# Splitting the first weight tile of the second MLP ahead of a norm, in a two-layer decoder on one core

## The chip, the cores and the metric

The kernel runs on one core of one Trainium2 chip. The metric is the device time of one execution in microseconds. The core has five engines, each with an instruction queue of its own: TensorE (PE; its weight loads are listed as PEld), VectorE (DVE), ScalarE (ACT), GpSimd (POOL) and SyncE (SP), which here issues most of the DMAs.

## The reference

A decoder of two layers works on 512 tokens of width 1024 (`x`), in fp32. Each layer has a mixer and an MLP, each behind an RMS norm whose scale and shift come from a conditioning vector (`mod`, six vectors of 1024 for each layer), and each added to `x` through a gate. Layer 0 mixes by pooling, layer 1 by a gated unit (SGU). The part around the change is the end of layer 1's mixer and the start of its MLP:

```python
    gated = u * mixed.reshape(B_, S_, SGU_WIDTH)
    return gated @ w_out
...
        x = x + g1[:, None, :] * y
        h = modulate(rmsnorm(x, norm_mlp_g[i]), sh2, sc2)
        x = x + g2[:, None, :] * sq_relu_mlp(h, mlp_w1[i], mlp_w2[i])
...
def sq_relu_mlp(h, w1, w2):
    return jnp.square(jax.nn.relu(h @ w1)) @ w2
```

## The kernel before

**Products in three parts.** Each fp32 operand of the large products is split into a high half (rounded, on ScalarE) and a low half (the rest, on VectorE); `mm3` (L174) then issues three matmuls, low weight by high input (L176), high weight by low input (L177), high by high (L178). A weight tile of 128 x 1024 (512 KB) is loaded by `raw4` (L153) and split by `split` (L164): high half `wh` by L167, low half `wl` by L168. `parts` (L590) does the same for inputs (L592 high, L593 low).

**Buffers.** Raw weight tiles, the tiles of the modulation columns (`ada`) and the scaled rows of a norm (`xs`) go round in one pool, `w4`, of three buffers: the fourth tile asked for takes the place of the first, and its load waits until that one has been read. `wh` and `wl` have five buffers each, PSUM has two pools of four banks (`ps`, `xz`).

**Order.** TensorE's instructions keep the order of the program. Those of ScalarE, VectorE, GpSimd and SP are put in order by the framework's scheduler, outside the first stage; on the chip each engine then works through its list in that order, and an instruction that waits holds up those behind it.

**The end of the mixer.** The tokens are in four tiles `t` of 128, the width in two halves `dh` of 512. For each `dh` the four blocks of `w_o` are loaded and split (`blocks`, L1028), and for each `t` 24 matmuls make a product `po` of 128 x 512. `gated` (L959) multiplies it by the gate (L964), adds it to `x` (L965), takes the sum of squares of the new half row on ScalarE (L969) and adds the sums (L973). After some of the token tiles `ada_tile` (L191) loads one modulation tile and reduces it on VectorE (L198, L183); GpSimd builds diagonals `dgu` from the results (L207).

**The norm.** `normed(hf, i, n)` (L980) norms 256 tokens, those of tiles 2hf and 2hf+1. GpSimd takes the power -1/2 (L223), ScalarE scales the two row tiles (L985, `xs`), TensorE turns them in 16 transposes (L992, `px`), VectorE and ScalarE apply scale and shift (L999, L997, into `h32`), and `parts` writes the two halves of the MLP's input `hb`, in four pairs of `k` (eight blocks `k` of 128 channels). `spill(hf)` (L1006) has GpSimd copy these tokens' `x` to memory (`xd`). For the first 256 tokens this stands in the gated output at `dh == 1`, after `t == 2`, so that TensorE works on `t == 3` while the first half is normed.

**The start of the MLP.** `first1` (L1130) loads and splits the first n = 4 tiles of `w1f` (tiles 0 to 3, each for 128 columns of the hidden width), multiplies them with the first 256 tokens, norms the second 256 after the third tile, then does tile 3's first half and all four tiles' second halves. Tiles 4 to 7 follow as units of `mlp` (L595): `f_prep` (L638) loads and splits them some units ahead. SP also loads the first tiles of the second weights there, `bt` and two of `b`, 1024 KB each (L761).

Of the kernel before, what the change touches and what calls it, by code (L numbers as in the profile page):

```python
# [78 lines left out]
def decoder_kernel(ctx: ExitStack, tc: tile.TileContext, xtok, vecs, rows, fgrow, ada0, adag, ada1, pool_w, w1s, w1, w1f, w1b, w2, w2e, w_v, w_u, w_o, wsT, lnp, bs, out):  # L79
# [23 lines left out]
    def f32(t):  # L103
        return t.bitcast(F32)
# [34 lines left out]
    def X(t):  # L139
        return x_[t // 2][:, t % 2]  # L140
# [8 lines left out]
    def mod(i, c):  # L149
        return mods[i][:, c : c + 1]  # L150


    def raw4(src):  # L153
        r = w4.tile([P, D], F32, name="raw", tag="w4")
        nc.sync.dma_start(r, src)
        return r
# [4 lines left out]
    def wpair():  # L161
        return wtile("wh"), wtile("wl")

    def split(r):  # L164

        h, l = wpair()
        A.activation(h, r, AF.Copy)  # L167
        V.tensor_tensor(l, r, f32(h), ALU.subtract)  # L168
        return h, l
# [63 lines left out]
    with (  # L233
# [67 lines left out]
        def rms():  # L301
            v0 = sm.tile([P, NT], F32, name="rv4", tag="rv4")
            V.tensor_scalar(v0, ss, RMS_EPS, None, ALU.add)
            rt.append(power(v0, NT))
# [270 lines left out]
    def ytile(name):  # L575
        return vy.tile([P, NT, D], F32, name=name, tag="y")
# [403 lines left out]
    def normed(hf, i, n):  # L980

        xs = []
        for r in range(2):
            t = w4.tile([P, D], F32, name="xs", tag="w4")
            A.activation(t, X(2 * hf + r), AF.Copy, scale=rms(2 * hf + r))  # L985
            xs.append(t)
        c = slice(256 * hf, 256 * hf + 256)
        for k in range(0, KD, 2):
            px = bank("px")
            for q in range(2):  # L990
                for r in range(2):
                    T.transpose(px[:, 256 * q + P * r : 256 * q + P * r + P], xs[r][:, P * (k + q) : P * (k + q) + P], ident)  # L992
            tt = h32[0][:, k : k + 2, c] if h32 else sm.tile([P, 2, 256], F32, name="tt", tag="tmp")
            for q in range(2):
                a, b = scl[i][n][:, k + q : k + q + 1], mod(i, c_sh(n, k + q))
                if q:
                    A.activation(tt[:, q], px[:, 256:512], AF.Identity, bias=b, scale=a)  # L997
                else:
                    V.tensor_scalar(tt[:, q], px[:, 0:256], a, b, ALU.mult, ALU.add)  # L999
            parts(H(slice(k, k + 2), c), tt)  # L1000
# [32 lines left out]
    with (  # L1033
        tc.tile_pool(name="lp", bufs=1) as lp,
        tc.tile_pool(name="up", bufs=8) as up,
        tc.tile_pool(name="gp", bufs=8) as gp,
        tc.tile_pool(name="ur", bufs=2) as ur,
    ):
        v4 = ytile("v")
        vt = [v4[:, t].rearrange("p (a b) -> p a b", a=2) for t in range(NT)]  # L1040
        lnt = lp.tile([P, 2, D], F32, name="lnt")
        wb = lp.tile([P, 2, HEADS, P], F32, name="wsbs")
        nc.sync.dma_start(lnt, lnp.rearrange("(o a b) -> o a b", o=1, a=2).to_broadcast([P, 2, D]))
        nc.sync.dma_start(wb[:, 0], wsT)
        nc.sync.dma_start(wb[:, 1], bs.rearrange("(o a b) -> o a b", o=1, a=HEADS).to_broadcast([P, HEADS, P]))
        G.affine_select(
            out=wb[:, 0], in_=wb[:, 0], compare_op=ALU.is_ge, fill=0.0, base=0, pattern=[[0, HEADS], [1, P]], channel_multiplier=-1
        )
        for ch in range(2):
            wv = blocks(w_v[ch])  # L1050
            for hf in range(2):
                ts = (2 * hf, 2 * hf + 1)
                pos = {t: bank("po", xz) for t in ts}
                for k in range(KD):
                    for t in ts:
                        mm3(pos[t], H(k, tok[t]), wv(k), k == 0, k == KD - 1)
                    if k == LATE and (ch, hf) == (0, 0):
                        normed(1, 1, 0)
                for t in ts:
                    A.activation(vt[t][:, ch], pos[t], AF.Gelu)  # L1060
        for t in range(NT):
            v = vt[t]
            stt = sm.tile([P, 2, V.BN_STATS_DIM], F32, name="stt", tag="stt")
            for ch in range(2):
                V.bn_stats(stt[:, ch, :], v[:, ch])
            ag = sm.tile([P, V.BN_AGGR_DIM], F32, name="ag", tag="ag")
            V.bn_aggr(ag, stt)
            r = rsqrt(ag[:, 1:2], 1.0, LN_EPS, 1)
            V.tensor_scalar(v, v, ag[:, 0:1], r, ALU.subtract, ALU.mult)
            for n, op in ((0, ALU.mult), (1, ALU.add)):  # L1070
                V.tensor_tensor(v, v, lnt[:, n].rearrange("p (a b) -> p a b", a=2), op)

        u, gt, wu = {}, {}, {}
        ex = [lambda: spread_cols(mods[1][:, c_g(0, 0) : c_g(0, 0) + KD])]
        ex += [lambda q=q: ada_tile(1, q, ada1[8 + q], get4) for q in range(24, 40)]

        def do_u(n):
            for q in range(n, min(n + 3, KD)):
                if q not in wu:
                    r = ur.tile([P, D], F32, name="ur", tag="ur")  # L1080
                    nc.sync.dma_start(r, w_u[q])
                    wu[q] = split(r)
            po = bank("po")
            wv = wu[n][0].rearrange("p (k c) -> p k c", k=KD), wu[n][1].rearrange("p (k c) -> p k c", k=KD)
            for k in range(KD):
                mm3(po, cut(wv, ALL, k), H(k, ALL), k == 0, k == KD - 1)
            u[n] = up.tile([P, S], F32, name="u", tag="u")
            A.activation(u[n], po, AF.Gelu)
            for _ in range(3):
                if ex:  # L1090
                    ex.pop(0)()

        def do_mix(hd):
            po = bank("po", xz)
            ch, c0 = hd // 4, P * (hd % 4)
            for t in range(NT):
                T.matmul(po[:, tok[t]], vt[t][:, ch, c0 : c0 + P], wb[:, 0, hd], start=True, stop=True)
            p4 = po.rearrange("p (a b) -> p a b", a=4)
            V.tensor_tensor(p4, p4, wb[:, 1, hd, :].unsqueeze(1).to_broadcast([P, 4, P]), ALU.add)
            V.tensor_tensor(u[hd], po, u[hd], ALU.mult)  # L1100
            h = gp.tile([P, S], F32R, name="gth", tag="gth")
            l = gp.tile([P, S], F32R, name="gtl", tag="gtl")
            A.activation(h, u[hd], AF.Copy)
            V.tensor_tensor(l, u[hd], f32(h), ALU.subtract)
            gt[hd] = h, l

        for op in "u0 u1 u2 u3 m0 u4 m1 m2 u5 m3 m4 u6 m5 u7 m6 m7".split():
            (do_u if op[0] == "u" else do_mix)(int(op[1]))
        ex += [lambda q=q: ada_tile(1, 40 + q, ada1[48 + q], get4) for q in range(8)]
        h_[0] = hparts(GAP)  # L1110
        h32.append(ytile("h32").rearrange("p t d -> p (t d)").rearrange("p (k s) -> p k s", k=KD))
        for dh in range(2):
            wo = blocks(w_o[dh])

            early = 6 if dh == 0 else KD
            pos = {}
            for t, ks in ((0, range(early)), (1, range(early)), (0, range(early, KD)), (1, range(early, KD)), (2, range(KD)), (3, range(KD))):
                if t not in pos:
                    pos[t] = bank("po", xz)
                for k in ks:  # L1120
                    mm3(pos[t], cut(gt[k], ALL, tok[t]), wo(k), k == 0, k == KD - 1)
                if KD - 1 in ks:
                    gated(t, S * dh, S, pos[t])
                    if ex:
                        ex.pop(0)()
                    if dh == 1 and t == 2:
                        normed(0, 1, 1)
                        spill(0)

    def first1(put):  # L1130
        n = 4
        wf = [split(raw4(w1f[f])) for f in range(n)]
        wf = [(h.rearrange("p (k c) -> p k c", k=KD), l.rearrange("p (k c) -> p k c", k=KD)) for h, l in wf]
        pos = [bank("po", xz) for _ in range(n)]
        for hf in range(2):
            c = slice(256 * hf, 256 * hf + 256)
            for f in range(n):
                for k in range(KD):
                    mm3(pos[f][:, c], cut(wf[f], ALL, k), H(k, c), k == 0, k == KD - 1)
                if f == n - 2 and hf == 0:  # L1140
                    normed(1, 1, 1)
                    spill(1)
        for f in range(n):
            put(f, pos[f])
        return n
# [109 lines left out]
```

## Time and profile before

| | |
|---|---|
| median of 3 runs | 876.26 us (875.87 to 877.03) |
| the profiled execution | 876.84 us |
| its span on the core | 875.1 us, 11762 instructions |
| mean granted TensorE clock | 0.998 |
| busy: PE, PEld, DVE, ACT, POOL | 98%, 84%, 78%, 51%, 6% of the span |
| DMA | 155.51 MB, mean 178 GB/s |

A row of the timeline gives the start (us from the span's start), the duration, the engine, the line, the operation, the tile written and the tiles read, how many such instructions are merged in the row, and in brackets the idle time before it and what ended it. A row of the stretches gives for PE, PEld, DVE, ACT and POOL the busy time and the number of instructions, then the granted clock, the share of the DMA engines that was busy, and GB/s. A row of the DMA list gives tile and source, the queue that issued it, how many, KB each, and the median us from issue to landing. In the costliest groups the last part is the engine's idle time in front of these instructions and what ended most of it.

### The profile page before, as it was taken

How to read it: one execution, taken by the hardware profiler on the slowest of the kernel's cores; microseconds unless marked ns; L12 is line 12 of the kernel's file. 1: busy time of each engine (PE TensorE's matmuls, PEld its weight loads, DVE VectorE, ACT ScalarE, POOL GpSimd, SP SyncE). 2: the span in 40 equal slices, each digit the busy share in tenths (PEclk: the TensorE clock that was granted, in tenths of full speed). 3: DMA queues.
4: the chain of work that ended last, by engine and by line, in shares of the span. 5: the costliest groups of instructions: out<-in, count | busy, mean ns of one | idle time of the engine just before them, and what ended most of it. 6: DMA issues, size and time to landing. Idle time of an engine off the chain costs nothing. (4 is left out here: it accounts for less than half of the span.)

```text
span 875.1 us, 11762 instructions
## 1 busy us (share of the span) xinstructions
PE 858.3 (98%) x4580; PEld 739.1 (84%) x4580; DVE 682.7 (78%) x893; ACT 449.6 (51%) x653; POOL 55.5 (6%) x75
## 2 busy tenths in 40 slices
PE   8999999999999999999999999999999999999996
PEld 7778888788888888888878888999999988889885
DVE  6889696788869876657798866776877798778965
ACT  5285755554444445337233336665765575556621
POOL 3000002000000000000410012000000000000001
PEclk9999999999999999999999999999999999999999
DMA  9969843553554442514658526817464547456312
GB/s 348 417 233 310 299 175 122 192 192 129 184 201 160 145 145 72 193 65 177 214 170 266 169 97 224 305 31 188 121 201 126 139 130 247 102 140 216 122 47 97
DMA packets 37789, 155.51 MB, mean 178 GB/s; under 512 B 4195, under 2 KB 4323, under 8 KB 32486
## 3 DMA queue, kind: packets, MB, share of 16 engines
q1 hardware_dynamic: 35282, 137.72, 43.9%
q0 software_dynamic: 2304, 16.78, 8.9%
q8 instruction: 36, 0.59, 0.3%
q10 hardware_dynamic: 148, 0.27, 0.1%
q14 instruction: 19, 0.16, 0.1%
HBM read 150.55 MB, written 4.19 MB: 177 GB/s over the span
## 5 line engine op out<-in xcount | busy, mean ns | idle before, releaser
L176 PE MATMUL po<-hb,wl 128*128 128x256 f32 (+1 forms) x624 | 209.3, 335 | 1.3 <-DVE wl L168 1.3
L178 PE MATMUL po<-hb,wh 128*128 128x256 f32 (+1 forms) x624 | 207.6, 333 | 0.0
L177 PE MATMUL po<-hb,wh 128*128 128x256 f32 (+1 forms) x624 | 207.6, 333 | 0.0
L168 DVE TENSOR_TENSOR wl<-raw,wh 128x1024 fp32r<-128x1024 f32 x107 | 130.9, 1224 | 39.4 <-ACT wh L167 39.0
L167 ACT ACTIVATE wh<-raw 128x1024 fp32r<-128x1024 f32 x107 | 112.7, 1057 | 64.8 <-PE pm L178 28.6
L178 PE MATMUL pm<-wh,oh 128*128 128x512 f32 x336 | 130.7, 389 | 0.0
L177 PE MATMUL pm<-wl,oh 128*128 128x512 f32 x336 | 130.7, 389 | 0.0
L176 PE MATMUL pm<-wh,ol 128*128 128x512 f32 x336 | 130.7, 389 | 0.0
L176 PEld LDWEIGHTS po<-hb,wl 128*128 128x128 f32 x624 | 117.1, 188 | 14.6 <-DVE wl L168 1.7
L177 PEld LDWEIGHTS po<-hb,wh 128*128 128x128 f32 x624 | 117.2, 188 | 13.0 <-issue 0.7
L178 PEld LDWEIGHTS po<-hb,wh 128*128 128x128 f32 x624 | 118.0, 189 | 11.9
L168 DVE TENSOR_TENSOR wl<-b,wh 128x1024 fp32r<-128x1024 f32 x60 | 73.0, 1221 | 24.7 <-ACT wh L167 24.7
L198 DVE SCALAR_TENSOR_TENSOR ada<-ada,cb 128x1024 f32<-128x1024 f32 x56 | 68.3, 1223 | 15.7 <-DMA ada<-in_ada 15.5
L178 PEld LDWEIGHTS pm<-wh,oh 128*128 128x128 f32 x336 | 63.0, 188 | 13.2
L176 PEld LDWEIGHTS pm<-wh,ol 128*128 128x128 f32 x336 | 63.1, 188 | 12.3
L177 PEld LDWEIGHTS pm<-wl,oh 128*128 128x128 f32 x336 | 63.0, 188 | 12.3
L167 ACT ACTIVATE wh<-b 128x1024 fp32r<-128x1024 f32 x60 | 63.0, 1055 | 13.0 <-PE pm L178 6.7
L630 ACT ACTIVATE g<-po 128x512 f32<-128x512 f32 x40 | 23.6, 599 | 75.7 <-PE po L178 73.8
L969 ACT ACTIVATE tmp<-x 128x512 f32<-128x512 f32 (+1 forms) x25 | 15.3, 612 | 63.0 <-DVE x L965 63.0
L857 DVE TENSOR_TENSOR y<-y,pm 128x512 f32<-128x512 f32 x68 | 43.6, 682 | 0.0
L176 PE MATMUL po<-as,wl 128*128 128x256 f32 x144 | 40.7, 283 | 2.9 <-DVE wl L168 1.9
L168 DVE TENSOR_TENSOR wl<-bt,wh 128x1024 fp32r<-128x1024 f32 x24 | 28.9, 1222 | 17.5 <-ACT wh L167 17.5
(211 smaller groups left out, 1491.0 us busy)
## 6 DMA issues: line engine op xcount, KB each, us to landing
ada<-in_ada SPq DMA_DIRECT2D x72, 512.0 KB, 3.3
b<-in_w SPq DMA_DIRECT2D x21, 1024.0 KB, 4.9
raw<-in_w SPq DMA_DIRECT2D x25, 512.0 KB, 3.9
raw<-in_w1b SPq DMA_DIRECT2D x24, 512.0 KB, 5.0
bt<-in_w POOLq DMA_DIRECT2D x9, 1024.0 KB, 8.3
raw<-in_w2e SPq DMA_DIRECT2D x16, 512.0 KB, 3.3
wh<-in_ada SPq DMA_DIRECT2D x9, 512.0 KB, 9.6
wl<-in_ada SPq DMA_DIRECT2D x9, 512.0 KB, 9.9
```

The source lines that it names most:

```text
L167: A.activation(h, r, AF.Copy)
L168: V.tensor_tensor(l, r, f32(h), ALU.subtract)
L176: T.matmul(o, wl, mh, start=first, stop=False, **kw)
L177: T.matmul(o, wh, ml, start=False, stop=False, **kw)
L178: T.matmul(o, wh, mh, start=False, stop=last, **kw)
L198: V.scalar_tensor_tensor(r, r, 1.0, cb, ALU.mult, ALU.mult, accum_out=pmv[i, b][:, j : j + 1])
L630: A.activation(t, po, AF.Relu)
L857: V.tensor_tensor(yt, yt, banks[hf], ALU.subtract if minus else ALU.add)
L969: A.activation(tmp, xt, AF.Square, scale=D**-0.5, accum_out=s[:, len(cs) : len(cs) + 1])
```

## The change

The load and split of tile 0 of `w1f` move from the start of `first1` into the loop of the gated output, at `dh == 1` after `t == 2`, in front of `normed(0, 1, 1)`. `first1` takes this tile from a list and loads and splits only tiles 1 to 3. No instruction of arithmetic is added or removed, and TensorE's order is unchanged. Since tile 0 now asks for its buffer of `w4` (and its `wh`, `wl`) ahead of the two `xs` tiles of that norm and of the last modulation tile, these move on by one place in the round, and the scheduler's order of SP, ScalarE and VectorE around them changes as well.

```diff
+        w1_first = []
         for dh in range(2):
             wo = blocks(w_o[dh])
...
                     if dh == 1 and t == 2:
+                        w1_first.append(split(raw4(w1f[0])))
                         normed(0, 1, 1)
                         spill(0)
 
     def first1(put):
         n = 4
-        wf = [split(raw4(w1f[f])) for f in range(n)]
+        wf = w1_first + [split(raw4(w1f[f])) for f in range(1, n)]
```

## The prediction

> **What bounds the kernel now.** I read the page first (busy shares, then the costliest groups), then the busy time by stretches of 10 us, then the timeline of each engine around the step that is moved.
>
> ```profile
> span 875.1 us, 11762 instructions
> PE 858.3 (98%) x4580; PEld 739.1 (84%) x4580; DVE 682.7 (78%) x893; ACT 449.6 (51%) x653; POOL 55.5 (6%) x75
> L176 PE MATMUL po<-hb,wl 128*128 128x256 f32 (+1 forms) x624 | 209.3, 335 | 1.3 <-DVE wl L168 1.3
> ...
> 530.00:540.00 10.00, 8.87 (x48) 7.25 (x46) 8.16 (x16) 7.42 (x14) 1.73 (x2) 1.00 0.62 229
> ...
> 550.00:560.00 10.00, 10.00 (x90) 10.00 (x89) 7.37 (x11) 7.38 (x13) 0.95 (x1) 1.00 0.97 334
> ...
> 700.00:710.00 10.00, 9.31 (x65) 8.54 (x64) 9.93 (x11) 8.93 (x13) 0.00 (x0) 1.00 0.52 105
> ```
>
> TensorE is busy 98% of the span, at the full granted clock (the 1.00 behind the busy times). A change elsewhere is worth only what it gives to or takes from TensorE's few gaps. Among the products by the second layer's first weights (the L176 group, out `po`, in `hb` and `wl`) there is one gap, 1.3 us, ended by the low half of a split weight tile. It lies in the stretch from 530 us, where TensorE has 8.87 of 10.00. The change aims at exactly this gap:
>
> ```profile
> 533.38 3.20 SPq L155 DMA_DIRECT2D raw<-in_w1f  x3
> ...
> 537.74 2.98 ACT L167 ACTIVATE wh<-raw 128x1024 fp32r<-128x1024 f32 x3
> ...
> 536.15 2.50 DVE L593 TENSOR_TENSOR hb<-h,hb 128x512 fp32r<-128x512 f32 x4
> 538.82 1.25 DVE L168 TENSOR_TENSOR wl<-raw,wh 128x1024 fp32r<-128x1024 f32 x1
> ...
> 538.26 0.39 PE L177 MATMUL po<-wl,gth 128*128 128x512 f32 x1
> 538.48 0.39 PE L178 MATMUL po<-wh,gth 128*128 128x512 f32 x1
> 540.13 0.38 PE L176 MATMUL po<-hb,wl 128*128 128x256 f32 x1 [1.26 <-DVE wl L168]
> ```
>
> Tiles 0 to 2 of w1f are requested at 533.38 us and after, when the transposes of the first 256 tokens give their buffers back. Their high halves come on ScalarE from 537.74, the low half of tile 0 on VectorE from 538.82 to 540.07, and TensorE, done with the gated output, waits for it until 540.13. The normed input itself (`hb`, L593) is complete at 538.65.
>
> **What the change removes.** Matmuls were 0.22 us apart before the gap (538.26 to 538.48), so without it tile 0 would start at 538.70 to 538.71: 1.42 us come off. For that, tile 0 has to be ready early, and the place where it now sits must not delay the norm.
>
> ```profile
> 518.16 0.08 DVE L198 DVE_READ_ACCUMULATOR ada<-ada,cb 128x1 f32 x1
> ...
> raw<-in_w1f SPq DMA_DIRECT2D x1, 512.0 KB, 3.2
> ...
> 523.57 0.63 ACT L969 ACTIVATE tmp<-x 128x512 f32<-128x512 f32 x1 [3.90 <-DVE x L965]
> ...
> 524.32 0.21 DVE L973 TENSOR_SCALAR sums<-sums 128x1 f32<-128x1 f32 x1 [0.85 <-ACT tmp L969]
> ...
> 525.29 1.15 ACT L985 ACTIVATE xs<-x,rr 128x1024 f32<-128x1024 f32 x1 [1.00 <-POOL rr L223]
> ...
> 527.77 0.63 ACT L969 ACTIVATE tmp<-x 128x512 f32<-128x512 f32 x1 [1.33 <-DVE x L965]
> ...
> 529.49 1.15 ACT L985 ACTIVATE xs<-x,rr 128x1024 f32<-128x1024 f32 x1 [1.00 <-POOL rr L223]
> ...
> 531.51 1.91 PE L992 MATMUL px<-ident,xs 128*128 128x128 f32 x16
> ...
> 535.01 1.22 DVE L198 SCALAR_TENSOR_TENSOR ada<-ada,cb 128x1024 f32<-128x1024 f32 x1
> ```
>
> In the built kernel tile 0's request stands on SP's queue behind three modulation tiles; it takes the buffer of the first of them, which VectorE has read by 518.24, so it goes out then and lands 3.2 us later by the row of the request at 533.38, at about 521.5. Its high half stands on ScalarE ahead of the square of 523.57, in 3.90 us of idle time; its low half on VectorE behind the addition that this square waits for (done by 523.5), so from 523.5 to 524.7. The sum of token tile 0 (L973), behind it, thus starts at 524.7 instead of 524.32, and its scaled rows end 0.4 us later, at 526.8, still ahead of the square at 527.77. Token tile 1 is untouched: its scaled rows end at 530.64, TensorE turns them from 531.51. Cost: nothing. If the request took 4 us more, all of it would show at 531.51. The last modulation tile takes tile 0's buffer and so goes out only at 524.7; landing 3.2 us later, at 527.9, it is there long before VectorE uses it at 535.01, so that costs nothing either.
>
> Tile 1 inherits tile 0's old place, low half done at 540.07. One tile of first-half products lasts 2.76 us (a third of 540.13 to 548.42, below), so TensorE wants it at 541.47. Tiles 2 and 3 take the next two places:
>
> ```profile
> 542.42 1.21 DVE L168 TENSOR_TENSOR wl<-raw,wh 128x1024 fp32r<-128x1024 f32 x1
> ...
> 543.16 2.44 ACT L985 ACTIVATE xs<-x,rr 128x1024 f32<-128x1024 f32 x2
> ...
> 548.42 1.91 PE L992 MATMUL px<-ident,xs 128*128 128x128 f32 x16
> ```
>
> VectorE works in order, so tile 2 is done before the row at 542.42, which is tile 3's and ends at 543.63, both ahead of need (544.2 and later), and the scaled rows of tokens 256 to 511 end at 545.60, where TensorE would now turn them at 548.42 - 1.42 = 547.00. Up to here the gain of 1.42 us stands.
>
> **What the change adds: a wait for tile 4.** Before, tile 3 had to wait for tile 0's buffer (requested 540.10) and tile 4 for tile 3's low half (requested 548.55). Now tile 3 is the third of the requests from 533.38, its low half is done at 543.63, and tile 4 goes out there, five microseconds earlier. With that the built order changes: tile 4's high half stands on ScalarE **ahead** of the four shift-and-scale steps of the second 256 tokens (L997), its low half on VectorE ahead of their four low parts (L593). Before, both stood behind them. The second half of the norm now waits for a transfer.
>
> ```profile
> 538.90 0.33 SPq L761 DMA_DIRECT2D bt<-in_w  x1
> 540.10 0.33 SPq L155 DMA_DIRECT2D raw<-in_w1f  x1
> 540.47 0.43 SPq L761 DMA_DIRECT2D b<-in_w  x1
> ...
> 548.55 0.33 SPq L155 DMA_DIRECT2D raw<-in_w1f  x1
> ...
> bt<-in_w SPq DMA_DIRECT2D x1, 1024.0 KB, 4.8
> ...
> b<-in_w SPq DMA_DIRECT2D x1, 1024.0 KB, 10.0
> ...
> raw<-in_w1f SPq DMA_DIRECT2D x2, 512.0 KB, 7.6
> ...
> xd<-x POOLq DMA_DIRECT2D x1, 1024.0 KB, 11.9
> ...
> q0 software_dynamic: 51, 0.42, 50.5%
> q1 hardware_dynamic: 54, 0.40, 47.5%
> ```
>
> The rows are SP's requests, then their times to landing; the last two are the two queues between 549 and 551 us. When does tile 4 land? Before, SP's queue held bt, tile 3 and b: 1024 + 512 + 1024 = 2560 KB, the first requested at 538.90, the last landed at 540.47 + 10.0 = 550.47. Now it holds bt, b and tile 4: again 2560 KB, bt still at 538.90 (it waits for TensorE's end of the gated output, which doesn't move), b right behind it, tile 4 at 543.65, when b is still moving. The same bytes in the same order of arrival, beside the same copy of x to memory: tile 4 lands at **550.47**. The bounds are far apart. If the copy kept out of the way, the 1536 KB behind bt (landed 543.7) would go at the best rate of a neighbouring microsecond, 438 GB/s, in 3.6 us: 547.3. The next two tiles of w1f, requested in the same traffic, took 7.6 us: 543.65 + 7.6 = 551.25. I take 550.47, since it is worked out for these bytes in this stretch.
>
> ```profile
> 542.00:543.00 1.00, 1.00 (x12) 1.00 (x11) 1.00 (x2) 0.47 (x1) 0.19 (x1) 1.00 1.04 438
> ...
> 549.63 1.02 ACT L997 ACTIVATE h<-px,mods,scl 128x256 f32<-128x256 f32 x2 [2.37 <-DVE h L999]
> ...
> 553.16 1.29 DVE L593 TENSOR_TENSOR hb<-h,hb 128x512 fp32r<-128x512 f32 x2 [0.66 <-ACT hb L592]
> ...
> 554.38 0.28 PE L177 MATMUL po<-hb,wh 128*128 128x256 f32 x1
> ```
>
> High halves follow each other by 0.96 us (2.98 less 1.06, over two), so L997 starts at 550.47 + 0.96 = 551.43 instead of 549.63: the norm is 1.80 us later. VectorE's 1.25 us for tile 4 end at 552.8, before the first low part could start, and add nothing. The third pair of low parts ended at 553.80 (553.16 and half of 1.29) and now ends at 555.60. TensorE used it at 554.38, with 0.58 us to spare; now it starts at 555.60, **1.22 us later than before**. In other words 1.42 us are gained and 2.64 given back: 2.06 before the first matmul of the second half, 0.58 at the third pair. Break-even is a landing at 549.25, the full gain one at 547.83 or earlier.
>
> Nothing behind takes up the shift. TensorE is full from 550 to 700 us; the gaps from 700 on, which VectorE ends, hang on this row, a copy of a product that ScalarE makes when TensorE has it, after which the order of the two kernels is the same:
>
> ```profile
> 664.44 0.60 ACT L860 ACTIVATE y<-pm 128x512 f32<-128x512 f32 x1 [3.41 <-PE pm L178]
> ```
>
> The profiled execution took 876.84 us (span 875.1 and 1.7 around it), 0.58 above the median of the runs, 876.26. The sum is 876.84 + 1.22 = 878.06 for a profile and 877.48 for the median: 877.5 us.
>
> **Rivals.** (a) *Tile 4 is on time*: it lands by 547.83, the norm of the second half doesn't wait, and the whole 1.42 us stay: 874.8 us; not slower. For it: bt alone took 4.8 us for 1024 KB, and the rate of 438 GB/s gives 547.3. Against it: b took 10.0 us in this very stretch. [...]
>
> (b) *Tile 4 is later still*: the copy of x, 542.81 to 554.7 by its 11.9 us, takes turns with SP's queue. From 549 to 551 the two queues moved 51 and 54 packets, turn and turn about. A row of tile 4 is 4 KB where a row of b is 8 KB, so in a fight packet by packet it would get a third, not half. With 7.6 us from request to landing (551.25) the sum is 1.22 + 0.78 = +2.0 us, 878.3; if the copy ended first (554.7), +5.4, 881.7. It decides from a landing of 551.0, where the loss is 1.75 us. [...]
>
> (c) *Tile 0 doesn't come early*: its request stays unlanded until the squares on ScalarE; then TensorE waits at 531.5 and the change gives nothing. Against it: a landing at about 521.5 leaves two microseconds before the square of 523.57. 876.3 to 878.
>
> **How the numbers follow.** 0.2% of 876 us is 1.75 us, about what a measurement of this kernel can tell from no change. Forecast, a landing between 548 and 551 (up to +1.75): 0.52. Rival (a): 0.22. Rival (b): 0.20, nearly all slower by over 0.2%. Rival (c): 0.02. For what I don't see, such as the gaps after 700 us closing or opening, 0.04, to either side. Since a landing near 550.9 is close to the limit, part of the forecast's chance goes to slower: faster 0.03, same 0.66, slower 0.31. The likeliest time is 877.5. The range runs from rival (a), 874.8, to a landing of about 552, +2.7, 879.0.
>
> **What would show it.** Right: no gap at the start of tile 0's products; tile 4's high half on ScalarE at about 550.5, ended by its DMA, ahead of L997; two gaps of TensorE near 551.6 and 555, about 2.06 and 0.6 us, ended by L593. Wrong: tile 4 landing before 548 (then I misjudged the queue, and the kernel is 1.4 us faster), a gap at 531 (the norm of the first half was delayed), or a gap between 560 and 700 us, where I see none.

## The result, and the profile after

The changed kernel takes 881.18 us (median; 880.26 to 883.9) where the kernel before, run beside it, takes 877.02: a ratio of 1.0048, interval 1.0033 to 1.0063, some 4.2 us slower. Run once more with other kernels it gave 1.0052 (1.0037 to 1.0067). I had forecast 877.5 from a median of 876.26, a loss of 1.2 us, and a range up to 879.0. One run of experiment 5, slow at 3273 us, is left out of its ratio below.

First the page of the changed kernel: its span, the busy shares and the two groups of products that now wait.

```profile
span 879.0 us, 11766 instructions
PE 860.8 (98%) x4580; PEld 741.5 (84%) x4580; DVE 682.4 (78%) x893; ACT 449.4 (51%) x653; POOL 55.6 (6%) x75
L176 PE MATMUL po<-hb,wl 128*128 128x256 f32 (+1 forms) x624 | 210.4, 337 | 1.9 <-ACT hb L592 1.9
L177 PE MATMUL po<-hb,wh 128*128 128x256 f32 (+1 forms) x624 | 208.8, 335 | 0.3 <-DVE hb L593 0.3
```

The span is 3.9 us longer. The wait for `wl` (1.3 us) is gone from the L176 group; a wait for the norm's `hb` has come in its place. But TensorE is also *busy* 2.5 us longer (860.8 against 858.3) with the same 4580 matmuls: only part of the loss is waiting. The timeline around the step:

```profile
522.14 1.06 ACT L167 ACTIVATE wh<-raw 128x1024 fp32r<-128x1024 f32 x1 [2.48 <-DMA raw<-in_w1f]
...
533.20 0.63 ACT L969 ACTIVATE tmp<-x 128x512 f32<-128x512 f32 x1 [2.64 <-DVE x L965]
...
538.47 0.39 PE L178 MATMUL po<-wh,gth 128*128 128x512 f32 x1
538.69 0.28 PE L176 MATMUL po<-hb,wl 128*128 128x256 f32 x1
...
543.64 0.33 SPq L155 DMA_DIRECT2D raw<-in_w1f  x1
...
551.32 1.06 ACT L167 ACTIVATE wh<-raw 128x1024 fp32r<-128x1024 f32 x1 [5.74 <-DMA raw<-in_w1f]
552.28 1.00 ACT L997 ACTIVATE h<-px,mods,scl 128x256 f32<-128x256 f32 x2
...
553.85 0.38 PE L176 MATMUL po<-hb,wl 128*128 128x256 f32 x1 [1.94 <-ACT hb L592]
554.58 0.39 PE L177 MATMUL po<-hb,wh 128*128 128x256 f32 x1 [0.34 <-DVE hb L593]
...
604.00 1.28 ACT L860 ACTIVATE y<-pm 128x512 f32<-128x512 f32 x2 [0.98 <-PE pm L178]
```

Tile 0 is early (high half at 522.14) and TensorE runs from the gated output into its products without a gap (538.47, 538.69), as forecast. Tile 4, requested at 543.64, holds ScalarE until 551.32, the shift-and-scale L997 stands behind it, and TensorE waits 1.94 + 0.34 us. The square at 533.20 and the copy at 604.00 frame what I call **the stretch** below. Before, the same two rows were:

```profile
533.22 0.63 ACT L969 ACTIVATE tmp<-x 128x512 f32<-128x512 f32 x1 [2.58 <-DVE x L965]
...
600.70 1.28 ACT L860 ACTIVATE y<-pm 128x512 f32<-128x512 f32 x2 [0.98 <-PE pm L178]
```

The stretch took 67.48 us before and 70.80 after: +3.32. The other 0.6 us come behind it, from gaps that were there before too. The forecast for the stretch was +1.22. What it lacked is in the busy time by stretches (the number after the five engines is the granted clock of TensorE):

```profile
550.00:560.00 10.00, 7.71 (x51) 7.31 (x50) 5.04 (x6) 5.83 (x11) 0.95 (x1) 0.83 0.96 300
...
555.00:556.00 1.00, 1.00 (x8) 1.00 (x7) 0.35 (x2) 1.00 (x3) 0.20 (x1) 0.60 0.89 315
556.00:557.00 1.00, 1.00 (x6) 1.00 (x6) 1.00 (x2) 0.27 (x1) 0.00 (x0) 0.50 0.93 225
557.00:558.00 1.00, 1.00 (x7) 1.00 (x6) 0.96 (x2) 0.00 (x0) 0.00 (x0) 0.50 1.14 160
558.00:559.00 1.00, 1.00 (x8) 1.00 (x8) 0.34 (x1) 0.00 (x0) 0.00 (x0) 0.70 0.74 139
```

Right behind the two waits TensorE runs at half clock. The four microseconds lack 0.40 + 0.50 + 0.50 + 0.30 = 1.70 us of full speed. In the trace the half clock is granted from 555.19 to 558.60 us, 3.41 us in all. Before, the same stretch had 1.00.

### The profile page after: what moved, and what is told of

It reads as the page before. It is cut to its first block, busy times and chain, and to the rows that moved or that the text cites. A ratio compares the mean times of both kernels' runs of the same rounds, so it can differ in the third digit from the quotient of the medians.

```text
span 879.0 us, 11766 instructions
## 1 busy us (share of the span) xinstructions
PE 860.8 (98%) x4580; PEld 741.5 (84%) x4580; DVE 682.4 (78%) x893; ACT 449.4 (51%) x653; POOL 55.6 (6%) x75
## 5 line engine op out<-in xcount | busy, mean ns | idle before, releaser
L176 PE MATMUL po<-hb,wl 128*128 128x256 f32 (+1 forms) x624 | 210.4, 337 | 1.9 <-ACT hb L592 1.9
L177 PE MATMUL po<-hb,wh 128*128 128x256 f32 (+1 forms) x624 | 208.8, 335 | 0.3 <-DVE hb L593 0.3
L177 PE MATMUL pm<-wl,oh 128*128 128x512 f32 x336 | 131.0, 390 | 0.0
L176 PE MATMUL pm<-wh,ol 128*128 128x512 f32 x336 | 130.9, 389 | 0.0
L176 PEld LDWEIGHTS po<-hb,wl 128*128 128x128 f32 x624 | 118.0, 189 | 15.1 <-ACT hb L592 2.1
L177 PEld LDWEIGHTS po<-hb,wh 128*128 128x128 f32 x624 | 118.0, 189 | 13.5 <-issue 0.7
L177 PEld LDWEIGHTS pm<-wl,oh 128*128 128x128 f32 x336 | 63.1, 188 | 12.5 <-DVE wl L168 0.2
L176 PEld LDWEIGHTS pm<-wh,ol 128*128 128x128 f32 x336 | 63.1, 188 | 12.3
L176 PE MATMUL po<-as,wl 128*128 128x256 f32 x144 | 40.7, 282 | 3.5 <-DVE wl L168 2.2
```

The source lines that it names most:

```text
L176: T.matmul(o, wl, mh, start=first, stop=False, **kw)
L177: T.matmul(o, wh, ml, start=False, stop=False, **kw)
```

## The experiments

Theory A says that the loss is tile 4's wait, with its clock step; its rivals put it elsewhere. After experiments 1 to 4 a second question came up: why removing the gap of 1.42 us gained nothing even where nothing was given back. The table holds, for the profiled execution of each kernel, TensorE's waits around the step, the lowest granted clock seen there in a stretch of a microsecond (of ten, where 1.00), and the stretch; the ratio is that of the timed runs.

| kernel | waits of TensorE, us | clock | stretch, us | ratio to before (interval) |
|---|---|---|---|---|
| before | 1.26 | 1.00 | 67.48 | 1 |
| changed | 1.94, 0.34 | 0.50 | 70.80 | 1.0048 (1.0033 to 1.0063) |
| changed, again | 3.02, 0.34 | 0.50 | 73.06 | 1.0052 (1.0037 to 1.0067) |
| tile 4 behind the norm | none | 1.00 | 67.62 | 0.9990 (0.9979 to 1.0002) |
| gap filled, 24 products | 0.33, 0.30 | 1.00 | 70.68 | 1.0004 (0.9993 to 1.0014) |
| copy of x later | 0.24, 0.31 | 1.00 | 67.54 | 0.9988 (0.9979 to 0.9997) |
| tile 4 ahead of b | 0.11, 0.34, 0.30 | 1.00 | 67.95 | 1.0009 (0.9997 to 1.0021) |
| short wait | 0.45 | 1.00 | 68.18 | 0.9987 (0.9976 to 0.9998) |
| middle wait | 0.72 | 1.00 | 67.04 | 0.9985 (0.9976 to 0.9994) |
| full wait | 1.25 | 1.00 | 67.58 | 0.9994 (0.9985 to 1.0004) |
| wait of 2 us | 2.24 | 1.00 | 68.56 | 1.0026 (1.0017 to 1.0035) |
| wait of 3 us | 2.90 | 0.50 | 70.82 | 1.0039 (1.0027 to 1.0051) |
| gap half filled, 12 products | 0.58, 0.34, 0.27 | 1.00 | 69.84 | 1.0017 (1.0008 to 1.0025) |
| before, low half in two pieces | 0.73 | 1.00 | 66.95 | 0.9994 (0.9985 to 1.0003) |

**1. Tile 4 behind the norm.** The changed kernel, but tile 4's split is issued behind the last split of the second norm.

```diff
+                r = raw4(w1[8 * c + f] if i == 0 else w1f[8 * c + f])
+                if (i, c, f) == (1, 0, 4):
+                    with tc.issue_after(norm_end["A"].ins), tc.issue_after(norm_end["V"].ins):
+                        return split(r)
```

> The changed kernel, but tile 4's high half is issued on ScalarE behind the last high half of the second 256 tokens' norm, its low half on VectorE behind the last low half; TensorE's, SP's and GpSimd's order stays. Theory A (the norm waits on ScalarE for tile 4's transfer, and TensorE's clock steps down behind the gap): no gap between tile 3's first half and the second halves, granted clock 1.00 from 550 to 560 us, L997 at about 548.2, and some 1.2 us less than before (ratio to before 0.9986), 5.4 less than the changed kernel. Rival B (the moved transfers and their crowding cost the time, whatever ScalarE's order): stays at about 881 us, ratio 1.005.

Ratio 0.9990; its interval holds no gain as well as the whole 1.42 us of the gap (a ratio of 0.9984). Rows of its timeline and stretches:

```profile
550.07 1.02 ACT L1003 ACTIVATE h<-px,mods,scl 128x256 f32<-128x256 f32 x2 [2.81 <-DVE h L1005]
...
553.97 1.06 ACT L167 ACTIVATE wh<-raw 128x1024 fp32r<-128x1024 f32 x1
...
550.00:560.00 10.00, 10.00 (x87) 10.00 (x86) 9.02 (x13) 8.69 (x15) 0.95 (x1) 1.00 0.87 288
```

With the norm (L1003, the same step as L997) ahead of tile 4, TensorE has neither wait nor half clock there, and the whole loss is gone: theory A stands. But there is no gap left at all in this stretch, and still it takes 67.62 us, 0.14 *more* than before with its gap. The busy time by groups of the products from 545 to 580 us says why, for the kernel before and then for this one:

```profile
L177 PE MATMUL po<-hb,wh 128*128 128x256 f32 x99 | 27.3, 276 | 0.0
```

```profile
L177 PE MATMUL po<-hb,wh 128*128 128x256 f32 x95 | 26.7, 281 | 0.0
```

The same product lasts 276 ns before and 281 ns here, and fewer fit into 35 us (99 and 95). By their starts in the trace they are 0.1133 us apart before and 0.1178 here. At 4.4 ns each (before rounding), the 377 products at the faster pace of the kernel before would take 1.66 us more at the slower one, as much as the 1.42 us of the gap and a little more.

**2. The gap filled.** The changed kernel with 24 products ahead of the second halves, overwritten later.

```diff
+            if hf:
+                for k in range(KD):
+                    for j in range(3):
+                        T.matmul(pos[0][:, c], cut(wf[0], ALL, k)[0], H(k, slice(0, 256))[0], start=True, stop=True)
```

> The changed kernel with 24 more matmuls of 256 columns between tile 3's first half and the second halves; they write the columns that tile 0's second half then overwrites, so TensorE computes 24 products for nothing, some 2.8 us of work in a gap of 2.7. Theory A with the clock as a cause of its own: the granted clock stays 1.00, the second halves run 0.113 us apart from the start, the third pair of low parts is waited for some 0.5 us, and the time is 1.2 us below the changed kernel (about 1.0034 of before). Rival C (the gap alone is the cost and the clock step lies in time that is waited anyway): no change against the changed kernel, 1.0048 of before, or more.

```profile
550.00:560.00 10.00, 9.36 (x76) 8.75 (x75) 5.52 (x10) 4.96 (x9) 0.95 (x1) 1.00 0.89 327
```

The clock stays at 1.00 where the changed kernel had 0.83, and the ratio falls from 1.0048 to 1.0004. That is more than the 1.7 us of the clock, and the ratio lies below both figures named ahead (1.0034 and 1.0048). Over the twelve runs the granted clock averages 0.9973, as in the kernel before beside it (0.9974), where the changed kernel has 0.9962 and, the second time, 0.9944. Three things blur the size. The scheduler also moved a few steps of ScalarE and VectorE of later units. In the profile tile 4 starts on ScalarE 19.01 us behind the square, 0.9 later than in the changed kernel, so the stretch (70.68) is hardly shorter. And the profiled execution is the longest of this kernel's runs (881.47, median 878.83): its trace has two more stretches of half clock, from 7.42 and from 31.31 us, far ahead of the step. So the half clock goes when TensorE is kept busy; what it costs isn't measured here.

**3. The copy of x later.** GpSimd's copy of the second 256 tokens waits for the last shift of the norm (a copy of one column); a load of `b` that GpSimd adds (L765) stays behind it, by lines not shown.

```diff
+        if h:
+            last = G.tensor_copy(ss[:, 0:1], h32[0][:, KD - 1, S - 1 : S])
+            with tc.issue_after(last.ins):
+                late.append(G.dma_start(xd[h], x_[h]))
+            return
```

> The changed kernel, but GpSimd copies the second half of x to memory only when the second norm's last shift is done (a one-column copy on GpSimd waits for it). Theory A2 (tile 4 lands late because it shares the DMA engines with this copy): tile 4, next in SP's queue when b lands at 546.2, lands by 547.6; ScalarE goes on by 547.8, the gap and the clock step are gone, the time is 1.2 us below before. Rival D (the queue of 2560 KB alone sets the landing, as the prediction had it): lands at 550.5, and the loss stays at about 1.3 us and the clock step with it, 1.003 of before.

The queues from 546.5 to 550.5 us, first of the kernel before, then of the changed one, then tile 4's row and SP's queue of this one:

```profile
q1 hardware_dynamic: 125, 0.89, 58.9%
q0 software_dynamic: 74, 0.61, 36.4%
```

```profile
q0 software_dynamic: 107, 0.75, 54.0%
q1 hardware_dynamic: 164, 0.80, 48.1%
```

```profile
549.17 1.06 ACT L167 ACTIVATE wh<-raw 128x1024 fp32r<-128x1024 f32 x1 [3.43 <-PE px L996]
...
q1 hardware_dynamic: 221, 1.29, 84.0%
```

In the changed kernel the copy (q0) takes half of the DMA engines' time (36.4% before), 0.75 MB, just while tile 4 is under way. Without it SP's queue moves 1.29 MB instead of 0.80, and tile 4 is there by 549.17, 2.15 us earlier. The row puts the end of ScalarE's wait down to the transposes; tile 4's last packet ended at 548.66, a microsecond later than expected, so its DMA may as well have ended it. The ratio, 0.9988, lies below the changed kernel's by 0.006. The copy of x is a cause of tile 4's lateness.

**4. Tile 4 ahead of b.** SP's two loads of `b` are issued behind tile 4's (the second behind tiles 5 to 7).

```diff
+                if i == 1 and c == 0 and not chain:
+                    with tc.issue_after(tile4[0].ins):
+                        nc.sync.dma_start(t, w2[i, c, r, n])
+                    return t
```

> The changed kernel, but on SP both b tiles are requested behind tile 4, the second behind tiles 5 to 7. Theory A2: bt lands at 543.4, tile 4, requested at 543.6, is alone but for the start of the copy and lands in 3.2 us, at 546.9; no gap, clock 1.00, 1.2 us below before. Rival B (crowding itself costs): the time stays at about 881 us.

```profile
549.39 1.06 ACT L169 ACTIVATE wh<-raw 128x1024 fp32r<-128x1024 f32 x1 [3.91 <-DMA raw<-in_w1f]
```

Tile 4 is there at 549.39, not at 546.9: with no load of `b` ahead of it, it still waits for the copy of x. From 543.5 to 546 us the copy's queue alone moves bytes, and tile 4's first row moves at 546.99. Two microseconds earlier than in the changed kernel are enough to bring the waits down to 0.75 us in all and to keep the clock at 1.00; ratio 1.0009. So the loads of `b` are a second cause: with either them or the copy out of the way, tile 4 comes some 2 us earlier.

**The changed kernel again.** It ran once more, beside experiments 5 to 7.

> The changed kernel once more, so that it stands beside the next three on one chip. Theory C (tile 4's wait, 2.7 us of gaps, plus about 1.6 us of half-clock matmuls behind it, plus what the later stalls add): 1.0045 to 1.005 of the kernel before, some 4 us. Rival (the clock step belongs to that one profiled execution and is rare otherwise): 1.002 to 1.003, some 2.5 us.

Ratio 1.0052. Its ScalarE and TensorE rows, and the products from 562 to 580 us:

```profile
552.04 1.06 ACT L167 ACTIVATE wh<-raw 128x1024 fp32r<-128x1024 f32 x1 [6.82 <-DMA raw<-in_w1f]
...
554.58 0.38 PE L176 MATMUL po<-hb,wl 128*128 128x256 f32 x1 [3.02 <-ACT hb L592]
...
L177 PE MATMUL po<-hb,wh 128*128 128x256 f32 x52 | 14.6, 281 | 0.0
```

Tile 4 landed later still, the first wait is 3.02 us, the clock fell to 0.50 again, and here the products stay at the slower pace (281 ns) behind it. The half clock is no accident of one execution, and the landing varies by a microsecond between executions.

**5 to 7. A wait put back.** Experiment 1 with one more product at the start of tile 0, overwritten later, that reads the first 128 columns of tile 1's low half. That half is written in a first piece of 256, 512 or 1024 columns, so TensorE waits more and more there and nowhere else.

```diff
-        V.tensor_tensor(l, r, f32(h), ALU.subtract)
+        for q in range(0, D, cut_at) if cut_at == S else [0, cut_at][: 1 + (cut_at < D)]:
+            c = slice(q, D if cut_at == 256 and q else q + cut_at)
+            V.tensor_tensor(l[:, c], r[:, c], f32(h)[:, c], ALU.subtract)
...
+        T.matmul(pos[0][:, 0:256], wf[1][1][:, 0], H(0, slice(0, 256))[0], start=True, stop=True)
```

> As the first experiment (tile 4 behind the norm), plus one product at the start of tile 0 that is overwritten and that reads the first columns of tile 1's low half, which is split in a first piece of 256 columns: TensorE waits there some 0.5 us. Theory P (the 128x256 products run 0.1133 us apart behind a wait of TensorE and 0.1176 us apart without one): if so short a wait is enough, the stretch from the last square of the gated output's tokens to the first copy of a product takes 66.6 to 66.8 us, some 0.8 us less than in the kernel before (67.5), ratio about 0.999; if it is not enough, 68.1 with products still 0.1176 us apart. Rival (the wait only costs its length, the pace has another cause): 68.1, 0.5 us more than the first experiment.

> The same with a first piece of 512 columns: TensorE waits some 0.8 us at the start of tile 0. Theory P: 66.8 to 67.0 us for the stretch if this wait sets the faster pace, about 0.6 us less than before; else 68.4. Rival: 68.4, 0.8 us more than the first experiment, at a pace of 0.1176.

> The same with the whole low half of tile 1: TensorE waits some 1.4 us at the start of tile 0, as in the kernel before. Theory P: the products run 0.1133 us apart again, the stretch takes 67.4 to 67.6 us, as in the kernel before and within 0.2 us of the first experiment, although TensorE stands still 1.4 us longer than there. Rival: 69.0 us, 1.4 us more than the first experiment and the kernel before, at a pace of 0.1176.

Each kernel's wait, and its group of products from 545 to 580 us (in these three L179 is the line that was L177):

```profile
539.59 0.39 PE L1146 MATMUL po<-hb,wl 128*128 128x256 f32 x1 [0.45 <-DVE wl L170]
...
L179 PE MATMUL po<-hb,wh 128*128 128x256 f32 x95 | 26.7, 281 | 0.0
```

```profile
539.52 0.38 PE L1146 MATMUL po<-hb,wl 128*128 128x256 f32 x1 [0.72 <-DVE wl L170]
...
L179 PE MATMUL po<-hb,wh 128*128 128x256 f32 x98 | 27.1, 276 | 0.0
```

```profile
539.84 0.39 PE L1146 MATMUL po<-hb,wl 128*128 128x256 f32 x1 [1.25 <-DVE wl L170]
...
L179 PE MATMUL po<-hb,wh 128*128 128x256 f32 x98 | 27.1, 276 | 0.0
```

With the full wait TensorE stands still 1.25 us longer than in experiment 1, and the stretch takes the same time (67.58 and 67.62 us). The rival, a wait that only costs its length, is out. A wait of 0.72 us buys the faster pace too and costs less: 67.04 us, and 0.9985 of the kernel before. This is the lowest ratio of the study, and its interval lies below both the kernel before and the changed one (experiments 3 and 5 come close to it). The wait of 0.45 us didn't change the pace in its profile (68.18 us, as its second case said), yet its timed runs came out at 0.9987, faster than the stretch allows. Whether other executions of it ran at the faster pace isn't known. The intervals of the ratios of experiments 1, 3, 5, 6 and 7 overlap, so which wait is best rests on one profile of each.

**8 and 9. A longer wait by itself.** The full wait, but the first 128 columns of tile 1's low half (768 in experiment 9) are written twice, the second time behind the first step of the gated addition, which had followed.

```diff
+        if cut_at == 1024 and again:
+            for q in [128]:
+                V.tensor_tensor(l[:, 0:q], r[:, 0:q], f32(h)[:, 0:q], ALU.subtract)
```

> As the experiment with the whole low half, but the first 128 columns of tile 1's low half are written a second time, behind the addition that follows, and the overwritten product waits for that: TensorE stands still some 2.0 us at the start of tile 0, and nowhere behind it. Theory K (a wait of TensorE of this length by itself brings a stretch at half clock behind it): the clock shows about 0.5 for some 3.4 us after the wait, the stretch from the last square to the first copy of a product takes 67.6 + 0.8 + 1.6 = 70.0 us, ratio 1.002 to 1.003. Rival (the half clock needs more than a single wait of 2.0 us, or has nothing to do with the wait): clock 1.00, 68.4 us, ratio about 1.0005. In both the products run 0.1133 us apart behind the wait, or 1.6 us more if not.

> The same with 768 columns written a second time: TensorE stands still some 2.75 us at the start of tile 0. Theory K: half clock for some 3.4 us behind it, 67.6 + 1.5 + 1.6 = 70.7 us for the stretch, ratio 1.003 to 1.004. Rival (the half clock in the changed kernel has another cause than the wait): clock 1.00 and 69.1 us, ratio 1.001 to 1.002.

The product that waits and the microsecond from 543 us, of experiment 8 and then of 9:

```profile
541.30 0.36 PE L1149 MATMUL po<-hb,wl 128*128 128x256 f32 x1 [2.24 <-DVE wl L173]
...
543.00:544.00 1.00, 1.00 (x11) 1.00 (x10) 1.00 (x2) 0.04 (x1) 0.00 (x0) 1.00 1.03 418
```

```profile
541.36 0.55 PE L1149 MATMUL po<-hb,wl 128*128 128x256 f32 x1 [2.90 <-DVE wl L173]
...
541.00:542.00 1.00, 0.64 (x3) 0.67 (x4) 1.00 (x3) 0.67 (x1) 0.00 (x0) 0.68 1.02 434
542.00:543.00 1.00, 1.00 (x7) 1.00 (x7) 1.00 (x2) 1.00 (x3) 0.62 (x1) 0.50 0.96 401
543.00:544.00 1.00, 1.00 (x6) 1.00 (x6) 1.00 (x1) 0.09 (x1) 0.00 (x0) 0.50 1.10 434
544.00:545.00 1.00, 1.00 (x8) 1.00 (x7) 0.21 (x2) 0.09 (x1) 0.57 (x1) 0.61 1.05 311
```

A wait of 2.90 us, with nothing else touched, brings the half clock; one of 2.24 us didn't in its profile. But the two differ in more than length. In each of the fourteen profiles the changes of the granted clock lie whole multiples of 3.413 us apart (before: at 5.32 and 872.30 us, 254 of them; changed: at 5.64, 555.19, 558.60 and 876.04 us, 161, 1 and 93), so they divide the span into equal intervals. Two of these of the changed kernel, then two of experiment 8:

```profile
551.78:555.19 3.41, 1.12 (x8) 0.80 (x7) 2.52 (x3) 3.41 (x8) 0.94 (x1) 1.00 0.92 368
555.19:558.60 3.41, 3.41 (x19) 3.41 (x18) 2.52 (x3) 1.08 (x3) 0.01 (x1) 0.50 0.97 219
```

```profile
536.46:539.88 3.42, 2.60 (x12) 1.82 (x10) 3.32 (x6) 3.42 (x6) 0.87 (x1) 1.00 0.79 296
539.88:543.29 3.41, 1.99 (x17) 2.02 (x18) 3.41 (x6) 2.85 (x5) 1.98 (x3) 1.00 0.88 320
```

Both waits of the changed kernel fall into one interval (3.41 us less 1.12 busy, so 2.29 idle), and the next one is at half clock. In experiment 9 the 2.90 us fall into one as well; in experiment 8 the wait lies across two, 0.82 and 1.42 us. Over all fourteen profiles, from 12 us to the end of TensorE's work, the five intervals with 2.02 to 2.90 us of idle time (2.29 in the changed kernel, 2.43 when it ran again, 2.90 in experiment 9) were each followed by one of half clock; none of the others, with 1.62 at most (1.44 before, 1.48 in the changed kernel), was. So theory K holds, and experiment 8 doesn't show that a wait of 2.24 us is safe. The sums of the stretch close: 67.58 + (2.24 - 1.25) = 68.57 for experiment 8 (measured 68.56), and 67.58 + (2.90 - 1.25) + (0.32 + 0.50 + 0.50 + 0.39) = 70.94 for experiment 9 (measured 70.82). In its timed runs experiment 8 lost 2.3 us, though, where its profile shows 1.1; that profile is the shortest of its runs, and over its twelve runs the granted clock averages 0.9966 where the kernel before beside it has 0.9976. One interval of half clock takes 0.002 off that average, so this is as if about every second run had one more.

**10. The gap half filled.** Experiment 2 with 12 products instead of 24.

```diff
-                    for j in range(3):
+                    for j in range(1 + k % 2):
```

> The changed kernel with 12 extra products, overwritten later, ahead of the second halves: they run inside TensorE's wait for tile 4 (2.1 to 3.2 us there) and take about 1.4 us of it, so they cost nothing and leave a wait of 0.7 to 1.8 us. Theory K: clock 1.00 throughout, 1.6 us less than the changed kernel, ratio 1.002 to 1.0035. Rival (the half clock is not set by how long TensorE stands still): clock near 0.83 in that stretch as in the changed kernel, ratio 1.0045 to 1.0052.

```profile
551.93 1.06 ACT L167 ACTIVATE wh<-raw 128x1024 fp32r<-128x1024 f32 x1 [5.77 <-DMA raw<-in_w1f]
...
554.47 0.38 PE L176 MATMUL po<-hb,wl 128*128 128x256 f32 x1 [0.58 <-ACT hb L592]
...
557.15 0.39 PE L177 MATMUL po<-hb,wh 128*128 128x256 f32 x1 [0.27 <-DVE hb L593]
...
550.00:560.00 10.00, 8.81 (x71) 8.20 (x70) 5.32 (x7) 5.96 (x11) 0.95 (x1) 1.00 0.97 314
```

In the profile this shows the clock most cleanly. Counted from the square (533.77 here, 533.20 in the changed kernel), tile 4 starts on ScalarE 18.16 us later where it was 18.12, and TensorE is back at the second half's products after 20.70 where it was 20.65: the lateness is the same, only TensorE isn't idle in between. The clock stays at 1.00 there and the stretch is 0.96 us shorter: 1.70 us of clock less the wait at the third pair, which reappears (557.15) because the products are no longer slow enough to hide it. In the timed runs the kernel gains more than that, 1.0050 to 1.0017 or 2.9 us; in the profile TensorE's gaps from 600 us on sum to 1.80 us, where the changed kernel's sum to 3.48. As in experiment 2 a few later steps had changed places. Over the twelve runs the granted clock averages 0.9963, less than in the kernel before beside it (0.9976) and not clearly more than in the changed kernel (0.9962 and, the second time, 0.9944). So half clock came in many of the other runs, and how much of the timed gain is the clock stays open.

**11. The kernel before, with its gap halved.** Tile 0's low half in two pieces of 512.

```diff
-        wf = [split(raw4(w1f[f])) for f in range(n)]
+        wf = [split(raw4(w1f[f]), 512 if f == 0 else D) for f in range(n)]
```

> The kernel before with one edit: tile 0's low half is written in two pieces of 512 columns, so that TensorE's wait at the start of tile 0 is some 0.6 us instead of 1.26. Theory P (a wait of 0.7 us was enough for the pace of 0.1133, one of 0.45 was not): between the two, so either 66.9 us for the stretch from the last square to the first copy of a product and a ratio of 0.9990 to 0.9995, or, if 0.6 us is too short, 68.5 us and 1.001. Rival (the pace has nothing to do with the wait): 66.9 us and the faster pace in any case.

```profile
539.63 0.39 PE L178 MATMUL po<-hb,wl 128*128 128x256 f32 x1 [0.73 <-DVE wl L170]
...
L179 PE MATMUL po<-hb,wh 128*128 128x256 f32 x98 | 27.1, 276 | 0.0
```

The wait falls from 1.26 to 0.73 us, the pace stays fast, and the stretch falls by the same 0.53 us, to 66.95. The ratio, 0.9994, agrees but isn't told apart from 1.

## Why the prediction was wrong

**Right: the place and the mechanism.** Tile 0 comes early at no cost, the gap at its start is gone, tile 4 holds up the second half of the norm by its DMA, and the change loses. Experiment 1 shows that the whole loss hangs on tile 4's place ahead of the norm: with tile 4 behind it the kernel is back at the time of before. Rival (c) didn't happen; rival (a), tile 4 on time, neither.

**The landing was mis-sized by 0.85 us.** I took 550.47 from the kernel before, "the same bytes in the same order of arrival, beside the same copy of x". The 2560 KB left out the second load of `b`, which stands right behind in SP's queue in both kernels: by 550.5 us that queue had moved 3.0 MB in either. What differed was the copy, which had moved 0.61 MB by then before and all of its 1.05 MB in the changed kernel; from 546.5 to 550.5 it took 54.0% of the engines' time against 36.4%. Rival (b) was nearest: a landing at 551.25 was its figure and ScalarE started at 551.32, though its 7.6 us were those of two other tiles, so that the hit is in part luck. Experiments 3 and 4 show that the copy and the loads of `b` each make tile 4 some 2 us late; what sets their turns stays open.

The runs don't settle how the two queues share the engines. In the kernel before, from 549 to 551 us, they moved 51 and 54 packets; in the changed kernel both move side by side (107 packets with 0.75 MB of the copy's queue and 164 with 0.80 MB of SP's, from 546.5 to 550.5 us); in experiment 4 SP's queue stands still for 2.5 us beside the copy. So a fight packet by packet, from which rival (b) worked out a third for tile 4, was my estimate.

Of the two waits I had 2.06 us, and 1.94 + 0.34 = 2.28 were measured idle, 2.71 by the starts of the products (551.63, 553.85 and 554.58, less 0.12 us for each step): +0.65.

**The step that failed is the assumption that a wait costs its length.** The sum counted gaps given and taken and left the granted clock at 1.00, as in every row that I had quoted. With 1.94 and 0.34 us of waiting so close together the clock halves for 3.41 us, which costs 1.70 us, less the 0.58 of the third pair, which is hidden behind them, so +1.12. In their profiles experiments 2 and 10 keep tile 4 as late, or later, and lose the half clock; experiment 9 makes the half clock with a wait alone. By the landing alone the loss would have been 1.22 + 0.85 = 2.07 us, inside the range. For the half clock 2.90 us in one wait were enough (experiment 9), and 1.94 + 0.34 us with work in between too.

**The gain was no gain in the profiles.** I took 1.42 us off for the gap. Experiments 1, 6 and 7 show that the gap had paid for itself: the products behind it run 0.1133 us apart, those that follow without a wait 0.1178. In the changed kernel this touches only the 94 products ahead of the new wait, since the pace is the faster one again behind it: 94 times 4.4 ns, +0.41. But it means that even a landing in time would hardly have brought the 1.42 us of rival (a): experiment 1 is the nearest to that case, and its stretch is 0.14 us longer than before. The timed ratios leave this open: those of experiments 1 and 3 are 0.9990 and 0.9988, and their intervals hold the whole gain of 1.42 us.

**The sum.** 1.22 forecast + 0.65 (landing) + 1.12 (clock) + 0.41 (pace) = 3.40; the stretch shows 3.32. The second and the last term aren't separate causes: TensorE waits for tile 4 at either pace, so what it loses ahead of that wait only shortens it. By the landing as such the sum is 1.22 + 0.85 + 1.12 = 3.19. The 0.6 us behind it, to 3.9, are mostly the gaps after 700 us, which I had called unchanged: they were a few tenths longer. These gaps differ between profiles in both directions, and I didn't find what sets them. In its second profile the changed kernel lost 5.58 us in the stretch, by a landing 1.1 us later and by a pace that stayed slow.

**The chances.** The chance of 0.31 for slower by over 0.2% sat nearly all on the landing. A further cost of 1.1 us, the half clock, was in no case, and where it comes the change is slower at any landing near my own. The upper end, 879.0, was a landing of 552 at full clock.

## What to carry to other kernels

A wait of TensorE is not priced by its length alone. When a change makes new waits close together, add the half-speed stretch that may follow (here 1.70 us lost behind 2.29 us of idle time within 3.41) and compare that with keeping TensorE busy on anything. When a change removes a short one, look at the mean duration of the products behind it before and after: in the profiles here a gap of 1.3 us was free, and cutting it to 0.7 was worth more than removing it. And before moving a load's step ahead of a norm, list what else is on the DMA engines at that moment; here a copy that nobody waited for, and loads that were wanted later, made tile 4 late.

## What the runs showed of the hardware

- **Half clock behind the intervals with the most idle time.** In each profile the changes of the granted clock lie multiples of 3.413 us apart. Intervals with 2.02, 2.16, 2.29 (the changed kernel), 2.43 (the same, again) and 2.90 us (experiment 9) of idle TensorE, in one wait or in several, were each followed by 3.41 us at a clock of 0.50; with 1.62 us or less there was none (in fourteen profiles, from 12 us on). A wait of 2.24 us that lay across two intervals had 1.00 behind it. No interval had between 1.62 and 2.02 us.
- **Two paces of the same product.** 128x256 products of fp32 halves run 0.1133 us apart (mean duration 276 ns) or 0.1178 (281 ns), at a granted clock of 1.00 in both. Without a wait ahead of them it was the slower pace every time; behind a wait it was the faster one in eleven profiles, down to waits of 0.24 and 0.31 us in experiment 3, and the slower one in two: behind 0.45 us in experiment 5, and behind 3.02 us in the second run of the changed kernel. In these profiles, then, the faster pace came only behind a wait, and the length of the wait didn't decide it. What does isn't visible in the trace, and stays open.
